# Output tiles of a two-layer hybrid transformer step: early tiles normed from DRAM by a task of their own, last head pair in token order

## The chip, the cores and the metric

The kernel runs on one core of one Trainium2 chip. The metric is the device time of one execution in microseconds (us), the median of several runs. Five engines work in parallel, each through its own instructions in order: TensorE (matrix products; PE in the profile, and PEld for its weight loads), VectorE (DVE), ScalarE (ACT), GpSimd (POOL) and SyncE (SP), which here only issues DMAs. Products write to PSUM, all else lives in SBUF, and DRAM is reached by DMA.

## The reference, cut to what matters

One inference step of a two-layer model on 1280 tokens: 256 context tokens and 1024 latent tokens, width 1024. In each layer

```
h   = rms_norm(x, g) * (1 + scale) + shift      # scale, shift, gate from SiLU(cond) @ mod_w
out = mixer(h)                                  # layer 0: attention and RWKV-7, layer 1: gated linear attention
x   = x + gate * (out @ w_out)
```

Layer 0 splits its projection into grouped-query attention (8 query heads, 2 key heads of 64, softmax; context tokens see 256 keys, latent tokens 1536 keys, 512 cached and 1024 latent) and a two-directional RWKV-7 recurrence; both are gated by SiLU, concatenated and put through one output projection `ev_w_out`. Layer 1 projects the new h to q, k, v, gate and decay inputs, runs chunked gated linear attention in both directions and projects with `od_w_out`. A last rms_norm gives the outputs, beside new keys, values and states. All is float32; the kernel writes each product as three products of a high and a low part (`hi*hi + lo*hi + hi*lo`).

## The kernel before, in words

**Tiles and groups.** The 1280 tokens are ten tiles of 128 (tiles 0 and 1 are the context) and three groups: group 0 is tiles 0 and 1, group 1 tiles 2 to 5, group 2 tiles 6 to 9.

**The planner.** The kernel is written as generator tasks in streams. `Sched.drive` runs all of them at build time: at each step it issues, among the instructions that stand next in some task, the one that by its cost numbers would start first (streams with a lower number first on ties). What it issues goes to the engines from one helper, line 357, so every row of the trace has L357, and each engine's order is fixed when the program is built. Tasks wait for conditions with `sch.until`, take buffer slots with `get` and give them back with `put`.

**Attention.** Twelve units, one for a head pair p4 (0 to 3) and a group, stand in a list (line 1668): for each head pair the groups 1, 2, 0. A unit finds the maxima of its scores (`mx`, sent through DRAM as `mr` into the row operand `QB`), multiplies `QA,KA` and `QB,KB` for scores, takes exponentials into `pt`, adds these up in `acc`, multiplies `pt,VO` for outputs and `acc,ones` for sums; their reciprocal `rcp` scales the gate path `ga`, which goes to the DRAM tensor `o`.

**Output tiles of layer 0** (`out_tile`, line 2191). A tile waits until its group is complete in `o` (attention and RWKV), loads its 128 tokens into the staging slot `wst` (one slot for the whole kernel, used for weight blocks as well), splits them into `oh` and `ol` (two slots each), and multiplies with the output weights `woh`, `wol`: 24 products for each block of 512 columns (tile 2: blocks of 256). At its first block it takes one of two slots `xt` and loads the residual x. `gt` is the product times the gate; `xt` becomes the sum, its squares go to `sq`, and `finish0` (line 2255) stores xt to the DRAM tensor `x1`. Three tiles may be under way at once, in the order of `TILES` (line 2272): tiles 2 to 9, then 0 and 1.

**The norm of the next layer.** `finish0` then waits for `flags["normed"]`, keeps its xt slot meanwhile, scales xt in place by the inverse root of `sq`, transposes it on TensorE (`ident,xt`), applies scale and shift into `xr` (one slot) and splits that into `h1hi`, `h1lo`. The room for these two is taken by attention, and `room_norm` opens it only when all twelve units are done. From then on the projections of layer 1 (`project`, line 1805) load their weights through wst into `whi`, `wlo` and multiply with h1hi, h1lo, group after group in the order 1, 2, 0.

Of the kernel before, what the change touches and what calls it, by code (L numbers as in the profile page):

```python
# [20 lines left out]
P = 128  # L21
DM = 1024
NK = DM // P
# [7 lines left out]
GROUPS = ((0, 256), (256, 512), (768, 512))  # L31
# [72 lines left out]
class Sched:  # L104
# [285 lines left out]
    def put(self, tag, tile):  # L390

        tile.slot.over = True
        self._release(tile.slot)
# [93 lines left out]
def tile_hybrid_dit_step(ctx: ExitStack, tc: tile.TileContext, I, C, O):  # L487
    nc = tc.nc
    sch = Sched(tc)
# [36 lines left out]
    def slots_in(pool0):  # L526
        def slots(tag, n, shape, dtype=F32, pool=None, fill=None):
            ts = [(pool or pool0).tile(shape, dtype, name=f"{tag}_{i}") for i in range(n)]
            for t in ts:
                if fill is not None:  # L530
                    G.memset(t, fill)
            sch.slots(tag, ts)
        return slots
# [190 lines left out]
    shared = slots_in(pool(ctx, "shared", side="right"))  # L724
    shared("wst", 1, [P, NK, P])
    shared("gt", 2, [P, 512])
    shared("sq", 6, [P, 4])
    shared("pj", 4, [P, 512], pool=pp)
    shared("a", 4, [P, 512], pool=pp)
    for tag in ("b", "po"):  # L730
# [934 lines left out]
    SLACK = 13  # L1665
    halves = [slice(64 * hh, 64 * hh + 64) for hh in range(2)]
    queries = {}
    units = [(p4, g) for p4 in range(4) for g in (1, 2, 0)]
    attended = [0, 0]

    def scores(g):
# [130 lines left out]
    heads = [dict(q={}, k={}, Vt={}, Sb={}, ready=set(), inner={}, back=set(), sf=None, out=0) for h in range(4)]  # L1802
    c128 = "p (c t) -> p c t"

    def project(cols, use):
        yield from sch.until(lambda: flags["normed"])
        yield from project_on(I["od_w_in"][0], H["hi"], H["lo"], cols, use, lambda g, a: normed[g] == GROUPS[g][1] // P, ORDER)

        def done():
            flags["units"] += 1  # L1810
        sch.then(done)
# [71 lines left out]
    def gates(h, u):  # L1883
        hd = heads[h]
        unit = 2 * h + u

        def use(g, t0, n, p):
            t1 = yield from get("gt", False)
            S.activation(out=t1[:, 0:n], in_=p, func=AF.Tanh, scale=0.5)
            V.scalar_tensor_tensor(out=t1[:, 0:n], in0=t1[:, 0:n], scalar=1.0, in1=p, op0=ALU.add, op1=ALU.mult)  # L1890
            D.dma_start(out=gg_d[g][:, unit, :], in_=t1[:, 0:n])
            put("gt", t1)

            def done():
                gated[g] += 1
            sch.then(done)
        yield from project([(0, OD_G + unit * P, P)], use)

    def step(h, d, tt, kt, Vt, j, cur, new):

# [290 lines left out]
    def out_tile(i, tt, src, finish):  # L2191
# [17 lines left out]
        copy(oh, ot)  # L2209
        pair(ol, ot, oh.bitcast(F32), ALU.subtract)  # L2210
        put("wst", ot)
        if i == 1:
            D.dma_start(out=xt, in_=src(tt))
        if tt in (0, 2):
# [2 lines left out]
            D.dma_start(out=gate, in_=gate_d[i][c:c + 1, :].to_broadcast([P, DM]))  # L2217
        yield from sch.until(lambda: (i, c) in gates_of)
        gate = gates_of[i, c]
        m = 256 if tt == 2 else 512  # L2220
        for b in range(DM // m):
            yield from sch.until(lambda: have[i] >= (b + 1) * m // P)
            cs = slice(b * m, (b + 1) * m)
# [25 lines left out]
        yield from finish(tt, xt, sq)  # L2249

    used = {}
    NW1 = 2
    MIXED = (8, 4)

    def finish0(tt, xt, sq):
        D.dma_start(out=x1_d[tt], in_=xt)
        yield from sch.until(lambda: flags["normed"])
        yield from norm_tile(1, tt, xt, sq, H["hi"], H["lo"])

        def done():  # L2260
            normed[0 if tt < 2 else (tt + 2) // 4] += 1
        sch.then(done)

    def finish1(tt, xt, sq):
        V.scalar_tensor_tensor(out=xt, in0=xt, scalar=sq[:, 2:3], in1=H["fg"], op0=ALU.mult, op1=ALU.mult)
# [8 lines left out]
    def room_proj():  # L2274
        yield from sch.until(lambda: all(x["over"] == 10 for x in sts))
        segs.close()
        out_pool(0, left, "wo0", 2)
        slots_in(pool(left, "xr", side="left"))("xr", 1, [P, NK, P])
        yield from move("b", "pj", 3)

    def room_norm():
# [70 lines left out]
    NAFTER = (0,0,0,6)  # L2352
    NGATE = 2
    def tiles(i):
        return ((out_tile(i, tt, (x_src, lambda t: x1_d[t])[i], (finish0, finish1)[i]) for tt in TILES), 3)

    def weights(i):
        return ((out_weights(i, (I["ev_w_out"], I["od_w_out"])[i][0], c) for c in range(8)), 2)
# [2 lines left out]
           ((states(h, g) for h in range(4) for g in (2, 1, 0)), 1, None, 0.15, 1.0),  # L2361
           ((outputs(h, g) for h in range(4) for g in ORDER), 2, None, 0.15, 1.0))
    sch.drive(([room_attn(), room_rwkv(), room_proj(), room_norm(), room_gla(), room_out(), room_more()], 7), *layer0_streams, *mixers,
              weights(0), tiles(0), *gla, (projections(), 2, None, 0.0, 1.5), weights(1), tiles(1))
    left.close()
    right.close()

# [82 lines left out]
```

## Time and profile before

| | before |
|---|---|
| median of 3 runs | 2095.14 us (2094.4 to 2097.18) |
| the profiled execution | 2095.28 us, span 2093.5 us |
| TensorE busy | 1997.0 us, 95% |
| VectorE, ScalarE, GpSimd busy | 1452.4, 1007.6, 289.9 us (69, 48, 14%) |
| weight loads on TensorE | 1557.7 us, 74% (beside the products) |
| TensorE busy from 1240 to 1470 us | 208.47 of 230 us |
| DMA | 219.56 MB, mean 105 GB/s |

The span is the time from the first to the last recorded instruction; the execution's own time has 1.8 us around it. A row of the trace gives start, duration, engine, line, operation and `output<-inputs` by the program's names; a bracket behind it is the engine's idle time ahead of the row and what ended it. Matmul rows overlap (a product of 512 columns shows 0.39 us, the next starts 0.23 us later), so the distance of starts is what one costs. The granted clock (PEclk) is a share of TensorE's upper level of 2.4 GHz; the lower level is 1.2 GHz.

### The profile page before, as it was taken

Reading aid. Unit: us, or ns where it says so; the run is one execution under the profiler, and the core shown is the slowest. Engines: PE = TensorE matmul, PEld = TensorE weight load, DVE = VectorE, ACT = ScalarE, POOL = GpSimd, SP = SyncE. Lnnn points to the kernel's source line nnn. Section 1 sums busy time; section 2 is a strip of 40 time slices with the busy share of each in tenths; the row PEclk is TensorE's granted clock in tenths of the full one; section 3 lists DMA queues with packets and bytes.
Section 4 is the critical chain, followed back from the end, with each engine's and each line's share of the span. In section 5 each row is a group of like instructions: output and inputs, shape, how many; then the busy total and the mean of one; then the engine's idle time right before and its main releaser. Section 6 shows DMA issues by size and latency. Waiting matters only on the chain.

```text
span 2093.5 us, 38539 instructions
## 1 busy us (share of the span) xinstructions
PE 1997.0 (95%) x14876; PEld 1557.7 (74%) x14876; DVE 1452.4 (69%) x2879; ACT 1007.6 (48%) x2184; POOL 289.9 (14%) x383
## 2 busy tenths in 40 slices
PE   6999999998999999999999999799999999999998
PEld 4878687886667777777776766578778888888886
DVE  4677866777887888778888987453575656564455
ACT  4454744553556655665656563333445454542111
POOL 2010200013221112121110020010121111110011
PEclk9999999999999999999999999899999999999999
DMA  8224342527513241323223224342102011115653
GB/s 297 71 101 159 138 164 81 179 91 238 170 54 103 81 143 59 97 74 111 78 68 88 67 70 143 95 146 73 50 14 64 28 50 29 49 31 165 192 170 112
DMA packets 215143, 219.56 MB, mean 105 GB/s; under 512 B 16480, under 2 KB 161232, under 8 KB 214960
## 3 DMA queue, kind: packets, MB, share of 16 engines
q1 hardware_dynamic: 214960, 217.10, 33.0%
q8 instruction: 117, 1.92, 0.4%
q14 instruction: 66, 0.54, 0.1%
HBM read 149.63 MB, written 67.39 MB: 104 GB/s over the span
## 4 chain that ended last, share of the span: by engine, by line
PE 52%; DVE 11%; issue 4%; ACT 3%; DMA 1%; POOL 0%; SPq 0%; POOLq 0%; DVEq 0%; ACTq 0%
PE a L357 26%; PE pj L357 26%; DVE QQ L357 2%; DVE LL L357 1%; DVE mx L357 1%; ACT QQ L357 1%; DVE TT L357 1%; DVE dec L357 1%; DVE gt L357 1%; DVE Z L357 1%; DVE y L357 1%; DVE GR L357 0%; DVE KX L357 0%; DVE GH L357 0%; DVE Ad L357 0%
## 5 line engine op out<-in xcount | busy, mean ns | idle before, releaser
L357 PE MATMUL pj<-hhi,whi 128*128 128x512 f32 (+1 forms) x672 | 241.1, 361 | 2.6 <-DVE whi L357 1.4
L357 PE MATMUL pj<-hhi,wlo 128*128 128x512 f32 (+1 forms) x672 | 240.4, 360 | 1.6 <-DVE wlo L357 1.6
L357 PE MATMUL pj<-hlo,whi 128*128 128x512 f32 (+1 forms) x672 | 241.3, 361 | 0.6 <-DVE hlo L357 0.6
L357 PEld LDWEIGHTS pj<-hhi,whi 128*128 128x128 f32 x672 | 128.9, 192 | 26.4 <-issue 3.7
L357 PEld LDWEIGHTS pj<-hhi,wlo 128*128 128x128 f32 x672 | 128.9, 192 | 24.0 <-issue 4.1
L357 PEld LDWEIGHTS pj<-hlo,whi 128*128 128x128 f32 x672 | 129.1, 192 | 23.7 <-issue 5.8
L357 POOL TENSOR_TENSOR acc<-acc,pt 128x512 f32<-128x512 f32 (+1 forms) x57 | 73.0, 1286 | 389.3 <-ACT pt L357 190.5
L357 PE MATMUL a<-h1hi,whi 128*128 128x512 f32 (+2 forms) x304 | 111.9, 369 | 0.0
L357 PE MATMUL a<-h1lo,whi 128*128 128x512 f32 (+2 forms) x304 | 111.0, 366 | 0.0
L357 PE MATMUL a<-h1hi,wlo 128*128 128x512 f32 (+1 forms) x296 | 109.9, 371 | 0.0
L357 PE MATMUL pj<-h1hi,whi 128*128 128x512 f32 (+2 forms) x296 | 108.4, 366 | 1.5 <-ACT h1hi L357 0.8
L357 PE MATMUL pj<-h1lo,whi 128*128 128x512 f32 (+2 forms) x296 | 108.4, 366 | 0.0
L357 PE MATMUL pj<-h1hi,wlo 128*128 128x512 f32 (+1 forms) x280 | 102.4, 366 | 0.0
L357 DVE TENSOR_TENSOR acc<-acc,pt 128x512 f32<-128x512 f32 (+1 forms) x127 | 90.6, 736 | 14.4 <-ACT pt L357 9.5
L357 PE MATMUL a<-pt,VO 128*64 128x512 f32 (+1 forms) x368 | 95.9, 605 | 0.0
L357 POOL TENSOR_SCALAR sq<-sq 128x1 f32<-128x1 f32 x70 | 19.9, 284 | 510.2 <-ACT gt L357 225.1
L357 DVE TENSOR_REDUCE mx<-pj 128x1 f32<-128x512 f32 (+1 forms) x118 | 75.4, 653 | 3.3 <-PE pj L357 3.1
L357 DVE TENSOR_REDUCE mx<-a 128x1 f32<-128x512 f32 x90 | 59.1, 669 | 10.8 <-PE a L357 10.7
L357 ACT ACTIVATE pt<-pj 128x512 f32<-128x512 f32 (+1 forms) x105 | 60.8, 597 | 10.2 <-PE pj L357 7.8
L357 PE MATMUL pj<-woh,oh 128*128 128x512 f32 (+1 forms) x160 | 61.5, 384 | 3.9 <-DVE oh L357 3.9
L357 PEld LDWEIGHTS a<-h1hi,whi 128*128 128x128 f32 (+1 forms) x304 | 56.9, 187 | 9.5 <-DVE gt L357 0.8
L357 PEld LDWEIGHTS pj<-h1hi,whi 128*128 128x128 f32 (+1 forms) x296 | 55.5, 188 | 11.2 <-ACT h1hi L357 1.2
(509 smaller groups left out, 5477.0 us busy)
## 6 DMA issues: line engine op xcount, KB each, us to landing
mw<-in_mod_w SPq DMA_DIRECT2D x24, 1024.0 KB
ws<-wk SPq DMA_DIRECT2D x32, 512.0 KB
wst<-in_ev_w_in SPq DMA_DIRECT2D x26, 512.0 KB
wst<-in_od_w_in SPq DMA_DIRECT2D x24, 512.0 KB
AR<-ws SPq DMA_DIRECT2D x40, 256.0 KB
BK<-ws SPq DMA_DIRECT2D x40, 256.0 KB
wst<-o SPq DMA_DIRECT2D x14, 512.0 KB
Vs<-vt SPq DMA_DIRECT2D x80, 64.0 KB
```

The costliest lines, as they stand in the source:

```text
L357: r = f(*a, **k)
```

## The change

Tiles that are finished before the room for h is open no longer keep their xt slot: `finish0` stores xt, gives the slot back and notes the tile in `rest`. A new task, `renorm`, waits for the room and goes through the tiles in token order; a noted tile it loads again from `x1` and norms. Tiles that finish later are normed at once as before. The last head pair's units and the tiles of layer 0 go in token order (groups 0, 1, 2). `project` waits until 8 tiles have split their activations, and the first two gate units (`NGATE`) project in the order 0, 1, 2. The tile with blocks of 256 columns is the first of its layer (tile 0 in layer 0, tile 2 in layer 1). `sq` has 12 slots in place of 6, `xr` 2 in place of 1.

```diff
@@ -724,7 +724,7 @@
     shared = slots_in(pool(ctx, "shared", side="right"))
     shared("wst", 1, [P, NK, P])
     shared("gt", 2, [P, 512])
-    shared("sq", 6, [P, 4])
+    shared("sq", 12, [P, 4])
     shared("pj", 4, [P, 512], pool=pp)
     shared("a", 4, [P, 512], pool=pp)
     for tag in ("b", "po"):
@@ -1665,7 +1665,7 @@
     SLACK = 13
     halves = [slice(64 * hh, 64 * hh + 64) for hh in range(2)]
     queries = {}
-    units = [(p4, g) for p4 in range(4) for g in (1, 2, 0)]
+    units = [(p4, g) for p4 in range(4) for g in ((1, 2, 0) if p4 < 3 else (0, 1, 2))]
     attended = [0, 0]
 
     def scores(g):
@@ -1802,9 +1802,9 @@
     heads = [dict(q={}, k={}, Vt={}, Sb={}, ready=set(), inner={}, back=set(), sf=None, out=0) for h in range(4)]
     c128 = "p (c t) -> p c t"
 
-    def project(cols, use):
-        yield from sch.until(lambda: flags["normed"])
-        yield from project_on(I["od_w_in"][0], H["hi"], H["lo"], cols, use, lambda g, a: normed[g] == GROUPS[g][1] // P, ORDER)
+    def project(cols, use, order=ORDER):
+        yield from sch.until(lambda: flags["normed"] and split[0] >= 8)
+        yield from project_on(I["od_w_in"][0], H["hi"], H["lo"], cols, use, lambda g, a: normed[g] == GROUPS[g][1] // P, order)
 
         def done():
             flags["units"] += 1
@@ -1894,7 +1894,7 @@
             def done():
                 gated[g] += 1
             sch.then(done)
-        yield from project([(0, OD_G + unit * P, P)], use)
+        yield from project([(0, OD_G + unit * P, P)], use, (0, 1, 2) if unit < NGATE else ORDER)
 
     def step(h, d, tt, kt, Vt, j, cur, new):
 
@@ -2209,6 +2209,10 @@
         copy(oh, ot)
         pair(ol, ot, oh.bitcast(F32), ALU.subtract)
         put("wst", ot)
+
+        def got():
+            split[i] += 1
+        sch.then(got)
         if i == 1:
             D.dma_start(out=xt, in_=src(tt))
         if tt in (0, 2):
@@ -2217,7 +2221,7 @@
             D.dma_start(out=gate, in_=gate_d[i][c:c + 1, :].to_broadcast([P, DM]))
         yield from sch.until(lambda: (i, c) in gates_of)
         gate = gates_of[i, c]
-        m = 256 if tt == 2 else 512
+        m = 256 if tt == 2 * i else 512
         for b in range(DM // m):
             yield from sch.until(lambda: have[i] >= (b + 1) * m // P)
             cs = slice(b * m, (b + 1) * m)
@@ -2249,17 +2253,38 @@
         yield from finish(tt, xt, sq)
 
     used = {}
+    split = [0, 0]
+    rest = {}
     NW1 = 2
     MIXED = (8, 4)
 
     def finish0(tt, xt, sq):
         D.dma_start(out=x1_d[tt], in_=xt)
-        yield from sch.until(lambda: flags["normed"])
+        if not flags["normed"]:
+            put("xt", xt)
+
+            def stored():
+                rest[tt] = sq
+            sch.then(stored)
+        else:
+            yield from norm0(tt, xt, sq)
+
+    def norm0(tt, xt, sq):
         yield from norm_tile(1, tt, xt, sq, H["hi"], H["lo"])
 
         def done():
             normed[0 if tt < 2 else (tt + 2) // 4] += 1
         sch.then(done)
+
+    def renorm():
+
+        yield from sch.until(lambda: flags["normed"])
+        for tt in range(10):
+            yield from sch.until(lambda: tt in rest or normed[0 if tt < 2 else (tt + 2) // 4] == (2, 4, 4)[0 if tt < 2 else (tt + 2) // 4])
+            if tt in rest:
+                xt = yield from get("xt")
+                D.dma_start(out=xt, in_=x1_d[tt])
+                yield from norm0(tt, xt, rest[tt])
 
     def finish1(tt, xt, sq):
         V.scalar_tensor_tensor(out=xt, in0=xt, scalar=sq[:, 2:3], in1=H["fg"], op0=ALU.mult, op1=ALU.mult)
@@ -2275,7 +2300,7 @@
         yield from sch.until(lambda: all(x["over"] == 10 for x in sts))
         segs.close()
         out_pool(0, left, "wo0", 2)
-        slots_in(pool(left, "xr", side="left"))("xr", 1, [P, NK, P])
+        slots_in(pool(left, "xr", side="left"))("xr", 2, [P, NK, P])
         yield from move("b", "pj", 3)
 
     def room_norm():
@@ -2352,7 +2377,7 @@
     NAFTER = (0,0,0,6)
     NGATE = 2
     def tiles(i):
-        return ((out_tile(i, tt, (x_src, lambda t: x1_d[t])[i], (finish0, finish1)[i]) for tt in TILES), 3)
+        return ((out_tile(i, tt, (x_src, lambda t: x1_d[t])[i], (finish0, finish1)[i]) for tt in (range(10), TILES)[i]), 3)
 
     def weights(i):
         return ((out_weights(i, (I["ev_w_out"], I["od_w_out"])[i][0], c) for c in range(8)), 2)
@@ -2361,7 +2386,7 @@
            ((states(h, g) for h in range(4) for g in (2, 1, 0)), 1, None, 0.15, 1.0),
            ((outputs(h, g) for h in range(4) for g in ORDER), 2, None, 0.15, 1.0))
     sch.drive(([room_attn(), room_rwkv(), room_proj(), room_norm(), room_gla(), room_out(), room_more()], 7), *layer0_streams, *mixers,
-              weights(0), tiles(0), *gla, (projections(), 2, None, 0.0, 1.5), weights(1), tiles(1))
+              weights(0), tiles(0), ([renorm()], 1), *gla, (projections(), 2, None, 0.0, 1.5), weights(1), tiles(1))
     left.close()
     right.close()
 
```

**The order on TensorE at the end of attention.** Before, these rows are the end of the last unit (64x256 outputs and sums of group 0), the norm transposes of a finished tile, and the first products of tile 4:

```order
L357 MATMUL a_145<-acc_3850,VO 64x256
L357 MATMUL a_145<-acc_3851,VO 64x256
L357 MATMUL a_145<-pt_3848,VO 64x256
L357 MATMUL a_145<-pt_3849,VO 64x256
L357 MATMUL pj_143<-acc_3850,ones_3830 64x256
L357 MATMUL pj_143<-acc_3851,ones_3830 64x256
L357 MATMUL pj_141<-ident,xt_12380 128x128 x4
L357 MATMUL a_146<-ident,xt_12380 128x128 x4
L357 MATMUL pj_142<-woh_12372,oh_12375 128x512
L357 MATMUL pj_142<-wol_12373,oh_12375 128x512
L357 MATMUL pj_142<-woh_12372,ol_12377 128x512
```

In the changed kernel the last scores, outputs and sums of the last unit (group 2) stand here, and behind them output products:

```order
L357 MATMUL pj_147<-QA_3842,KA_3832 128x512
L357 MATMUL pj_147<-QB_3846,KB_3834 128x512
L357 MATMUL pj_149<-QA_3843,KA_3832 128x512
L357 MATMUL pj_149<-QB_3847,KB_3834 128x512
L357 MATMUL a_151<-pt_3854,VO 64x512
L357 MATMUL a_151<-pt_3855,VO 64x512
L357 MATMUL pj_148<-acc_3856,ones_3836 64x512
L357 MATMUL pj_148<-acc_3857,ones_3836 64x512
L357 MATMUL a_153<-woh_12368,oh_12371 128x512
L357 MATMUL a_153<-wol_12369,oh_12371 128x512
L357 MATMUL a_153<-woh_12368,ol_12373 128x512
```

Before, the last sums are followed at once by transposes. Now 86 products of 512 columns (rows 9373 to 9458: both blocks of tile 2, the first of tile 3, 14 products of tile 4's first) stand between the last sums and the first transposes. The place where these begin, tile 2's norm between products of tile 4 and tile 3:

```order
L357 MATMUL a_152<-woh_12368,oh_12371 128x512
L357 MATMUL a_152<-wol_12369,oh_12371 128x512
L357 MATMUL pj_147<-ident,xt_12376 128x128 x4
L357 MATMUL pj_149<-ident,xt_12376 128x128 x4
L357 MATMUL a_153<-woh_12368,oh_12372 128x512
```

The next transposes, of tile 0 loaded again, stand 34 products later (row 9495); those of tiles 3, 1, 4, 5, 6, 7, 8 and 9 follow at rows 9516, 9548, 9556, 9610, 9669, 9712, 9772 and 9825.

**The order on SP around the room.** Before: activations to wst for tiles 3 and 4 (o01 is group 1), a weight block of layer 1 (in_od_w_in), the stores of tiles 2 and 3, the last attention output (o00), and the residuals, store and activations that follow:

```order
L357 DMA wst_0_131<-o01_106 128x8x128 x2
L357 DMA wst_0_131<-in_od_w_in 128x8x128
L357 DMA x1_2_116<-xt_1_12380 128x1024
L357 DMA x1_3_117<-xt_0_12379 128x1024
L357 DMA o02_107<-ga_0_3852 128x512
L357 DMA ga_0_3852<-ga3_96 128x256
L357 DMA xt_1_12380<-in_x_sample 128x1024
L357 DMA o00_105<-ga_0_3852 128x256
L357 DMA xt_0_12379<-in_x_sample 128x1024
L357 DMA x1_4_118<-xt_1_12380 128x1024
L357 DMA wst_0_131<-o01_106 128x8x128
L357 DMA xt_1_12380<-in_x_sample 128x1024
```

In the changed kernel, from the store of tile 0 on (x1_0):

```order
L357 DMA x1_0_114<-xt_1_12376 128x1024
L357 DMA xt_1_12376<-in_x_sample 128x1024
L357 DMA gate_0_12370<-gate0_69 128x1024
L357 DMA wst_0_131<-o01_106 128x8x128
L357 DMA x1_1_115<-xt_0_12375 128x1024
L357 DMA o02_107<-ga_0_3858 128x512
L357 DMA xt_0_12375<-x1_0_114 128x1024
L357 DMA wst_0_131<-o01_106 128x8x128
L357 DMA x1_2_116<-xt_1_12376 128x1024
L357 DMA xt_1_12376<-in_x_sample 128x1024
L357 DMA x1_3_117<-xt_1_12376 128x1024
L357 DMA wst_0_131<-o02_107 128x8x128
```

The stores of tiles 0 and 1 stand ahead of the last attention output (o02), and the reload of tile 0 right behind it; tile 1's (row 550) follows two rows after this piece. The first weight block of layer 1 has moved to row 556, behind the activations of tile 7. These two are the only reloads.

## Rows read from the trace of the kernel before

**Rows 1.** The page: span, busy times, and the 40 slices (tenths).

```profile
span 2093.5 us, 38539 instructions
PE 1997.0 (95%) x14876; PEld 1557.7 (74%) x14876; DVE 1452.4 (69%) x2879; ACT 1007.6 (48%) x2184; POOL 289.9 (14%) x383
...
PE   6999999998999999999999999799999999999998
...
PEclk9999999999999999999999999899999999999999
```

**Rows 2.** Windows from 1240 to 1470: busy of each engine, PEclk, DMA share, GB/s.

```profile
1260.00:1280.00 20.00, 16.42 (x59) 8.44 (x60) 16.01 (x27) 8.52 (x18) 0.00 (x0) 0.83 0.68 203
...
1340.00:1350.00 10.00, 7.82 (x22) 5.77 (x23) 4.74 (x7) 3.40 (x9) 0.00 (x0) 0.54 0.54 158
...
1410.00:1420.00 10.00, 7.63 (x32) 5.96 (x31) 5.50 (x8) 4.78 (x10) 0.00 (x0) 0.83 0.37 84
...
sum 230.00, PE 208.47 PEld 155.91 DVE 125.86 ACT 87.56 POOL 17.03; mean PE 20.85 PEld 15.59 DVE 12.59 ACT 8.76 POOL 1.70
```

**Rows 3.** TensorE's waits, 1230 to 1520: total us, times, longest us.

```profile
PE pj L357 <- DVE xt L357: 9.9, 2, 7.5
PE a L357 <- DMA QB<-mr: 3.0, 1, 3.0
PE pj L357 <- DVE mx L357: 2.0, 1, 2.0
PE pj L357 <- ACT xt L357: 2.0, 1, 2.0
...
PE a L357 <- DVE rcp L357: 1.0, 1, 1.0
PE pj L357 <- ACT h1hi L357: 0.8, 1, 0.8
...
PE pj L357 <- ACT whi L357: 0.7, 1, 0.7
PE pj L357 <- ACT gsq L357: 0.6, 1, 0.6
```

**Rows 4.** Timeline of TensorE around the longest wait: start us, us, instruction.

```profile
1333.12 0.40 PE L357 MATMUL pj<-woh,ol 128*128 128x512 f32 x1
1341.01 1.12 PE L357 MATMUL pj<-ident,xt 128*128 128x128 f32 x4 [7.50 <-DVE xt L357]
...
1344.11 0.80 PE L357 MATMUL pj<-woh,oh 128*128 128x512 f32 x1 [1.13 <-DVE oh L357]
...
1349.31 0.39 PE L357 MATMUL pj<-woh,ol 128*128 128x512 f32 x1
...
1352.07 0.39 PE L357 MATMUL pj<-woh,ol 128*128 128x512 f32 x1
```

**Rows 5.** Timeline of VectorE beside it.

```profile
1338.00 1.22 DVE L357 TENSOR_TENSOR wlo<-wst,whi 128x1024 fp32r<-128x1024 f32 x1
1340.20 0.75 DVE L357 TENSOR_SCALAR xt<-xt,sq 128x1024 f32<-128x1024 f32 x1 [0.98 <-DMA x<-xt]
1343.36 0.69 DVE L357 CAST oh<-wst 128x1024 fp32r<-128x1024 f32 x1 [2.41 <-DMA wst<-o]
```

**Rows 6.** Timeline of SP: when DMAs were issued.

```profile
1337.51 0.32 SPq L357 DMA_DIRECT2D x<-xt  x1
1339.25 0.53 SPq L357 DMA_DIRECT2D wst<-o  x1
...
1405.76 0.33 SPq L357 DMA_DIRECT2D gate<-gate  x1
```

**Rows 7.** The chain that ended last, around 1405 us: start us, us, what.

```profile
1405.04 0.70 DVE gt L357
...
1406.49 5.42 DMA x<-xt
...
1412.03 0.76 DVE xt L357
```

## The prediction

> **What bounds the kernel now.** I read the page's totals first: TensorE is busy 1997.0 us of a span of 2093.5 us, no other engine comes near, and the line of 40 slices shows nearly full slices from the second on, with one clear hole in the middle and a granted clock that falls only there [rows 1]. So the kernel is bound by TensorE, the change does not alter its number of products, and all it can move is that hole. Second I cut the stretch 1240 to 1470 us into windows: TensorE is busy 208.47 of 230 us, so 21.53 us are idle [rows 2]. The same windows have a clock below full, and that is a second loss: 0.17 x 20 = 3.4 us in 1260:1280 and 0.17 x 10 = 1.7 us in 1410:1420 [rows 2]. In 1340:1350, mostly at the lower level (1.2 GHz), I take it from the products: the 24 from 1344.11 to 1352.07 need 1352.07 - 1344.11 + 0.23 = 8.2 us, while 12 steps from 1349.31 to 1352.07 give 0.23 us each at the upper level, 5.5 us for 24; loss 2.7 us [rows 4]. The eight transposes ahead of them lose under 1 us more, which I leave out. Together 21.5 + 3.4 + 1.7 + 2.7 = 29.3 us can be won here and next to nothing elsewhere.
>
> Third, who ends the idle times [rows 3]: two waits on the scaled residual tile xt make 9.9 us, a handover between two attention units 3.0 + 2.0 us (the round trip of its maxima through DRAM), the start of the norms when the room opens 2.0 us, and small ones. The longest, 7.5 us, runs from 1333.5 to 1341.01 [rows 4]. It looks like one late vector instruction, but three things stand in a row. Tile 4's last product starts at 1333.12; its x1 store is issued at 1337.51 [rows 6]; the scaling, in place, starts at 1340.20 when the store has landed [rows 5]. And TensorE has no other product to do, because tile 5's activations were loaded only at 1339.25 [rows 6] and cast at 1343.36 [rows 5]: the one staging slot wst held a weight block of the next layer until its low part was made at 1338.00 [rows 5]. So the same gap ends in two waits, 7.5 us and then 1.1 us at 1344.11 [rows 4], and taking away the first alone would have left TensorE waiting to 1344 for the second. Behind both is one fact: tiles 2 and 3 are finished, hold both xt slots, and cannot be normed before the last attention unit frees the room for h; tile 4 then starts with nothing beside it.
>
> **The change, part by part.** (1) *Tiles finished early give their xt slot back* (`finish0`, `renorm`), and tiles 0 and 1 come first. In the new order only tiles 0 and 1 finish before the room opens, so only two reloads are added, 512 KB each, and nothing on TensorE. The reload of tile 0 stands on SP's queue behind the last attention output. After the last attention product 86 output products follow before the first transposes, which are tile 2's: 86 x 0.23 = 19.8 us [rows 4]. Tile 0's transposes come 34 products later. A load of this size took 1343.36 - 1339.25 = 4.1 us from issue to first use [rows 5, 6], so both reloads lie under other work. The 19.8 us also replace what was missing: room, moves of buffers and norm set-up now pass under products that need no room.
>
> The Trainium skill, "DMA: Bandwidth & Descriptors", section "Anatomy of one DMA — SWDGE (gpsimd) path", speaks against a trip through DRAM: each DMA has a fixed cost of about 2.0 us, mostly the receipt of the write, and "this can cause a surprisingly long delay especially when the write target is HBM". The trace agrees in kind: the x1 stores here take 2.7 us and once 5.42 us until the scaling may go [rows 5 to 7]. By the page's figure a store and a reload would add an estimated 4 us and the movement for each of two tiles if nothing covered them; the order puts more than 19 us of products over both, so my sum has nothing for them.
>
> (2) *The weight blocks of the next layer wait until 8 tiles have been split* (`split[0] >= 8`). This takes the weight out of wst's way: on SP the activations of tiles 4 to 7 now come ahead of the first such weight. The 1.1 us wait and the part of the 7.5 us behind it have no cause any more.
>
> (3) *What is late next: the norm of each tile.* From a tile's last product to its transposes run gate, add, store, scale. Tile 4: 1333.5 to 1341.01, 7.5 us [rows 4]; tile 9: 1405.04 to 1412.03 + 0.76, 7.8 us, in which the store took 5.42 us, issued right behind a 512 KB gate load of 1405.76 [rows 6, 7]. With a store of 2.7 us the latter chain is 5.1 us. In the new order I count the products between each tile's last and its transposes: 38 for tile 2 (8.7 us); 28 and one set of transposes (1.0 us) for tiles 3 and 4 (7.4 us); 34 for tile 5 (7.8); 43 for tile 6 (9.9); tile 7 about 6.7, tile 8 7.4, tile 9 6.9 us, with 256-column products at half the price. At 5.1 us for all chains the stalls are 0; at 7.8 us they are 0 + 0.4 + 0.4 + 0 + 0 + 1.1 + 0.4 + 0.9 = 3.2 us. The gate rows of the latent tokens are now loaded early, which takes away what delayed tile 9; but two reloads are in the traffic: I take 1.8 us, about the sum at tile 4's 7.5 us.
>
> (4) *Head pair 3 in token order.* The last attention unit is now one of 512 tokens and 12 key tiles in place of 256 tokens and 2. The handover remains, in the same form: maxima, their trip through DRAM, the first scores. It cost 2.0 + 3.0 us [rows 3] and 3.4 us of clock [rows 2], 8.4 us. Bounds: 0, if the two tiles of products that are now at hand fall into it, and 8.4. The order shows some 94 products of 256 columns right behind the unit's first eight scores, but not in the wait itself; I take 5.2 us. The unit's end (last exponential, last sums) cost 0 to 2.0 us (the wait at the room [rows 3]) plus a reciprocal of about 1 us; bounds 0 and 3.0, taken 2.0.
>
> (5) *Gate units 0 and 1 in the order (0, 1, 2), two xr slots, 12 sq slots.* They decide what stands beside the last norms. The waits on h1hi (0.8) and whi (0.7) and on gsq (0.6) [rows 3] I leave as they are: 2.1 us. After the last transposes 72 products of 512 columns and some smaller ones stand ahead of the first that wait for the decay, 72 x 0.23 = 16.6 us at least, so the last norm is not exposed.
>
> Sum of what is left: 5.2 + 2.0 + 1.8 + 2.1 = 11.1 us, against 29.3. Gain 18.2 us. The profiled execution took 2095.28 us (the span of 2093.5 and 1.8 around it), 0.14 us above the median of 2095.14, which I neglect: 2095.2 - 18.2 = **2077.0 us**. With all terms at their lower bounds 2.1 us stay, gain 27.2, 2068; with all at their upper bounds 8.4 + 3.0 + 3.2 + 2.1 = 16.7, gain 12.6, 2082.6.
>
> **Rivals.** *A, the residual slots become the new wait.* Two xt slots now carry ten tiles and two reloads. One of them serves tile 2, tile 3, the reloaded tile 1 and tile 5: from tile 2's transposes load 4.1, chain 7.8, reload, scale and transposes 5.9, load 4.1, chain 7.8: 29.7 us. TensorE has in that stretch 140 products and five sets of transposes, 32.2 + 5 = 37 us. For: each load waits for another tile's transposes, and SP issues in order, so the store of tile 3 stands ahead of the load for tile 4. Against: 7 us of slack. If loads and stores that overlap take twice as long (the store did: 5.42 against 2.7), the slot is 29.7 + 3 x 4.1 + 2.7 = 44.7 us, 7.7 us late, and the clock falls once more, about 2.7 us: 2077.0 + 10.4 = **2087**.
>
> *B, the hole moves.* The 86 products are only two and a half tiles' worth that now stand behind the attention instead of under its last unit, so that unit may run uncovered: its scores wait for exponentials as the old handover did. For: the old last unit had 8 scores of 256 columns and the tiles around it. Against: 94 + 48 products are still placed between its steps. A second handover (8.4 us) and tail (3.0) beyond my terms, with a clock loss of 3.4: 2077.0 + 14.8 = **2092**, no change.
>
> *C, slower: TensorE starves at several tiles.* Mechanism: the reload of an early tile takes an xt slot before its room on TensorE comes, the next tile's residual is not there, its sums fill the PSUM slots and the products behind stand still. Price of one such stop, from the gap of before: 7.5 + 1.1 + 2.7 = 11.3 us [rows 3, 4]. It decides from two on, which use up the gain: 2077.0 + 22.6 = **2099.6**; three would give 2111. For: the planner knows no such landing times as 5.42 us. Against: two reloads only, and the slack under A.
>
> **How the numbers follow.** Forecast (2068 to 2084, its own range) 0.70; A 0.15; B 0.08; C 0.07. About 0.2%, 4.2 us, is what a measurement of this kernel can tell from no change. The forecast and A are faster by more, B within, C beyond on the other side: faster 0.85, same 0.08, slower 0.07. The range is 2067 to 2090: it takes in the forecast's bounds and A.
>
> **What would show it.** In the new profile TensorE should be busy above 95% in every 100 us between 1200 and 1500, with no wait over 3 us behind xt, and the clock near full from the last attention product on; the reloads should be issued within 5 us of the last attention output and land long before their transposes. The handover's waits on mx and QB should be the largest that are left, together 3 to 4 us. A shows as waits of TensorE for xt whose vector instruction waits for a load; B as waits for pt, acc or mr around 1250 to 1300; C as two or more gaps above 7 us with a clock of 1.2 GHz behind each. If the idle time went as forecast and the time did not, the clock terms are wrong.

## The result and the profile after

The changed kernel takes 2078.68 us (median of 5 runs, 2075.22 to 2080.1) against 2094.49 us of the kernel before beside it: ratio 0.9922, 95% interval 0.9909 to 0.9936, so 15.8 us faster (13.4 to 19.1). The forecast was 2077.0.

The profiled execution has a span of 2077.7 us, 15.8 us less than before [rows 1]. The page:

```profile
span 2077.7 us, 38540 instructions
PE 1991.9 (96%) x14876; PEld 1554.9 (75%) x14876; DVE 1453.5 (70%) x2877; ACT 1007.2 (48%) x2181; POOL 296.1 (14%) x388
```

The hole of before is nearly gone: TensorE's busy share from 1300 to 1500 us is above 98%. What is left lies ahead of 1300, where 91.67% misses the prediction's sign of more than 95% in every 100 us. Windows (columns as in [rows 2]):

```profile
1200.00:1300.00 100.00, 91.67 (x621) 58.84 (x621) 85.07 (x143) 52.00 (x107) 16.52 (x9) 0.98 0.31 94
1300.00:1400.00 100.00, 98.18 (x484) 79.61 (x482) 56.36 (x84) 36.43 (x84) 10.88 (x18) 1.00 0.46 147
1400.00:1500.00 100.00, 98.80 (x542) 79.00 (x541) 43.74 (x72) 38.93 (x73) 7.73 (x11) 1.00 0.23 68
```

TensorE's waits from 1230 to 1520 us, which answer to [rows 3]:

```profile
PE pj L357 <- DVE mx L357: 5.3, 3, 3.2
PE a L357 <- DVE ol L357: 1.0, 1, 1.0
PE a L357 <- DVE QQ L357: 0.8, 1, 0.8
PE pj L357 <- ACT gsq L357: 0.6, 1, 0.6
PE pj L357 <- DVE xt L357: 0.6, 1, 0.6
```

The 9.9 us behind xt are 0.6, the 2.0 us at the room and the 3.0 us behind QB are gone, and the maxima (mx) have grown from 2.0 to 5.3 us, where the prediction's sign was 3 to 4 us on mx and QB together.

The reloads are covered. SP issues the load of tile 0 (xt<-x) 1.1 us after the last attention output (o<-ga), and that of tile 1 only 32 us after it, at 1356.92:

```profile
1324.70 0.32 SPq L357 DMA_DIRECT2D o<-ga  x1
1325.76 0.32 SPq L357 DMA_DIRECT2D xt<-x  x1
...
1335.91 0.61 SPq L357 DMA_DIRECT2D x<-xt  x1
...
1356.92 0.32 SPq L357 DMA_DIRECT2D xt<-x  x1
```

VectorE scales tile 0 at 1329.74, 4.0 us after the issue, tile 1 at 1361.76, 4.8 us after, and tile 2 at 1341.39, 5.5 us after its store was issued (1335.91), the link that the prediction read at 2.7 and 5.42 us:

```profile
1329.74 0.76 DVE L357 TENSOR_SCALAR xt<-xt,sq 128x1024 f32<-128x1024 f32 x1 [0.69 <-DMA xt<-x]
...
1341.39 0.75 DVE L357 TENSOR_SCALAR xt<-xt,sq 128x1024 f32<-128x1024 f32 x1 [5.52 <-DMA x<-xt]
...
1361.76 0.75 DVE L357 TENSOR_SCALAR xt<-xt,sq 128x1024 f32<-128x1024 f32 x1
```

On TensorE the last sums start at 1320.80, tile 2's transposes wait 0.55 us, and tile 0's come at 1350.87, 20 us after it was scaled. Tile 1's come at 1363.55, 1.0 us after it was scaled: no wait, but the prediction's sign (both reloads issued within 5 us of the last attention output, and landed long before their transposes) holds for tile 0 alone:

```profile
1320.80 1.13 PE L357 MATMUL pj<-acc,ones 128*64 128x512 f32 x3
...
1342.20 1.09 PE L357 MATMUL pj<-ident,xt 128*128 128x128 f32 x8 [0.55 <-DVE xt L357]
...
1350.87 0.38 PE L357 MATMUL pj<-ident,xt 128*128 128x128 f32 x2
...
1363.55 0.60 PE L357 MATMUL pj<-ident,xt 128*128 128x128 f32 x4
```

**A ruler for the rest.** The two programs give TensorE the same order up to head pair 3's first products. I measure from the last easily found products ahead of these (products of the recurrence, pj<-Z,TT followed by a<-TT,Z; before: 1155.00) to the first product of 64 rows of the next layer's decay inputs (before: 1463.25); the same number of products lies ahead of that one in every run. The kernel before needs 308.25 us for this stretch, the changed kernel 1448.31 - 1158.39 = 289.92: a gain of 18.3 us. In this profile 3.4 us were lost ahead of it, in code that is the same, and 0.9 us won behind it: 18.3 - 3.4 + 0.9 = 15.8.

### The profile page after: what moved, and what is told of

Same layout as the page of the kernel before. It is cut to its first block, busy times and chain, and to the rows that moved or that the text cites. A ratio compares the mean times of both kernels' runs of the same rounds, so it can differ in the third digit from the quotient of the medians.

```text
span 2077.7 us, 38540 instructions
## 1 busy us (share of the span) xinstructions
PE 1991.9 (96%) x14876; PEld 1554.9 (75%) x14876; DVE 1453.5 (70%) x2877; ACT 1007.2 (48%) x2181; POOL 296.1 (14%) x388
## 4 chain that ended last, share of the span: by engine, by line
PE 55%; DVE 11%; issue 2%; ACT 2%; DMA 1%; SPq 0%; POOL 0%; POOLq 0%; DVEq 0%; ACTq 0%
PE a L357 31%; PE pj L357 24%; DVE QQ L357 2%; DVE mx L357 1%; DVE LL L357 1%; ACT QQ L357 1%; DVE TT L357 1%; DVE Z L357 1%; DVE dec L357 1%; DVE gt L357 1%; DVE y L357 0%; DVE GR L357 0%; DVE KX L357 0%; DVE acc L357 0%; DVE TR L357 0%
## 5 line engine op out<-in xcount | busy, mean ns | idle before, releaser
L357 PE MATMUL a<-h1hi,whi 128*128 128x512 f32 (+3 forms) x448 | 162.2, 363 | 0.0
L357 PE MATMUL a<-h1lo,whi 128*128 128x512 f32 (+3 forms) x448 | 161.7, 362 | 0.4 <-DVE h1lo L357 0.4
L357 PE MATMUL a<-h1hi,wlo 128*128 128x512 f32 (+1 forms) x424 | 153.7, 362 | 0.0
L357 PE MATMUL a<-woh,oh 128*128 128x512 f32 (+1 forms) x248 | 91.8, 370 | 2.8 <-DVE oh L357 2.8
L357 PEld LDWEIGHTS a<-h1hi,whi 128*128 128x128 f32 (+1 forms) x448 | 83.3, 186 | 13.3 <-issue 0.4
L357 PEld LDWEIGHTS a<-h1lo,whi 128*128 128x128 f32 (+1 forms) x448 | 83.3, 186 | 13.2 <-DVE h1lo L357 0.8
L357 PE MATMUL a<-woh,ol 128*128 128x512 f32 (+1 forms) x248 | 91.5, 370 | 1.7 <-DVE ol L357 1.7
L357 PE MATMUL a<-wol,oh 128*128 128x512 f32 (+1 forms) x248 | 91.5, 369 | 0.0
L357 PEld LDWEIGHTS a<-h1hi,wlo 128*128 128x128 f32 x424 | 80.1, 189 | 11.2 <-DVE wlo L357 0.4
L357 ACT ACTIVATE pt<-pj 128x512 f32<-128x512 f32 (+1 forms) x123 | 68.7, 593 | 35.4 <-PE pj L357 31.8
```

The costliest lines, as they stand in the source:

```text
L357: r = f(*a, **k)
```

## The experiments

All ratios are to the kernel before on the same chip; the stretch is from the run's one profile.

| kernel | median, us | ratio, 95% interval | stretch, us |
|---|---|---|---|
| before | 2093.85 to 2096.18 | 1 | 308.25 |
| changed | 2078.68 | 0.9922, 0.9909 to 0.9936 | 289.92 |
| e1 renorm alone | 2121.04 | 1.0114, 1.0099 to 1.0130 | 330.77 |
| e2 wait for split tiles alone | 2095.05 | 1.0004, 0.9994 to 1.0015 | 307.87 |
| e3 order alone | 2080.92 | 0.9929, 0.9915 to 0.9942 | 292.52 |
| e4 changed, no renorm | 2081.40 | 0.9927, 0.9914 to 0.9939 | 291.68 |
| e5 units' order alone | 2094.33 | 0.9997, 0.9987 to 1.0008 | 304.48 |
| e6 tiles' order alone | 2097.47 | 1.0021, 1.0012 to 1.0031 | 309.92 |
| e7 before, split wait, 4 tile tasks | 2088.70 | 0.9975, 0.9966 to 0.9984 | 300.69 |
| e8 changed, maxima 20 ahead | 2079.11 | 0.9936, 0.9922 to 0.9951 | 295.60 |
| e9 changed again | 2077.31 | 0.9917, 0.9903 to 0.9930 | 289.98 |
| e10 changed, weights' low parts on VectorE | 2074.99 | 0.9911, 0.9899 to 0.9924 | 287.10 |
| e11 changed, no split wait | 2075.56 | 0.9912, 0.9899 to 0.9925 | 290.14 |
| e12 changed, maxima 16 ahead | 2080.75 | 0.9929, 0.9917 to 0.9942 | 291.56 |

The kernel before has one profile too. In 11 of the 13 runs its 308.25 us gives a larger gain than the ratio does, by 1.5 us on the mean of all 13, so gains read from the stretch may be too large by about that (an estimate). e5's 3.8 us is the clearest case: its interval allows 2.7 at most.

**e1: renorm alone.** The kernel before with `finish0`, `renorm` and 12 sq slots of the changed one:

```diff
-        yield from sch.until(lambda: flags["normed"])
+        if not flags["normed"]:
+            put("xt", xt)
...
-              weights(0), tiles(0), *gla, ...
+              weights(0), tiles(0), ([renorm()], 1), *gla, ...
```

> The kernel before with one part of the change alone: tiles finished early go to DRAM and are normed by a task of their own (renorm, 12 sq slots); units, tiles and projections keep the old order, the next layer's weights may still take wst. In the order 240 output products now stand ahead of the last sums and 80 behind them before the first transposes, but four tiles (2 to 5) are reloaded, and their transposes come at the very end, five sets in a row with hardly a product between. Theory (the hole closes where products are at hand, and opens where a chain load-scale-transposes has none): the wait of 7.5 us at the room goes, but a new stop of 8 to 13 us stands at the end of the norms; gain 3 to 8 us, 2087 to 2092. Rival 1 (the held xt slots are the whole cause): nearly the full gain, 12 to 18 us. Rival 2 (the gain is the order of units and tiles): 0 to 2 us.

Slower by 1.1%, 22.5 us in the stretch. The sign was against every theory, the mechanism was the first one's. Timeline of TensorE at the end of the norms:

```profile
1430.83 1.11 PE L357 MATMUL pj<-ident,xt 128*128 128x128 f32 x4 [5.81 <-DVE xt L357]
...
1436.56 1.11 PE L357 MATMUL pj<-ident,xt 128*128 128x128 f32 x4 [3.76 <-ACT xt L357]
...
1443.72 0.98 PE L357 MATMUL pj<-ident,xt 128*128 128x128 f32 x4 [3.49 <-DVE xt L357]
...
1447.96 1.09 PE L357 MATMUL pj<-ident,xt 128*128 128x128 f32 x4 [2.41 <-DVE xt L357]
...
1453.88 1.22 PE L357 MATMUL pj<-h1hi,whi 128*128 128x512 f32 x2 [3.98 <-ACT h1hi L357]
```

Five waits, 19.5 us: tile 1's own chain, then four early tiles that come back through two slots, with no product left to stand beside them (the granted clock is 0.51 from 1430 to 1440 us, nearly all at its lower level of 1.2 GHz). Two more waits, 7.0 us on oh at 1343.91 and 6.9 us on xt at 1399.70, are, as I read them, the old hole, moved. Releasing the slots is no gain by itself.

**e2: the split wait alone.** The kernel before with the count of split tiles and

```diff
-        yield from sch.until(lambda: flags["normed"])
+        yield from sch.until(lambda: flags["normed"] and split[0] >= 8)
```

> The kernel before with one part alone: projections wait until 8 tiles are split, so no weight block of the next layer holds the staging slot wst. Tile 5's products can then follow tile 4's at once, 18 of them ahead of tile 4's transposes (4.1 us) in place of none. Theory (two causes in a row behind the 7.5 us wait, wst being the second): the 7.5 + 1.1 us shrink to 3 to 4 us and the clock drop behind them mostly goes; gain 5 to 8 us, about 2088. Rival 1 (held xt slots are the whole cause): 1 us, the 1.1 us wait alone. Rival 2 (order): 0 to 2 us.

No change. The wait of 7.5 us at tile 4 is gone (its transposes come at 1347.24 without a wait), but other waits took its place; the waits of this run:

```profile
PE pj L357 <- DVE xt L357: 4.9, 3, 4.1
PE pj L357 <- ACT oh L357: 3.3, 1, 3.3
PE a L357 <- DMA QB<-mr: 2.8, 1, 2.8
PE pj L357 <- ACT whi L357: 2.2, 1, 2.2
```

The wait of 1.1 us on oh is now 3.3 us, and tile 5's low parts (ol) are late by 1.2 us:

```profile
1339.33 0.79 PE L357 MATMUL pj<-woh,oh 128*128 128x512 f32 x1 [3.31 <-ACT oh L357]
...
1414.23 1.12 PE L357 MATMUL pj<-ident,xt 128*128 128x128 f32 x4 [4.14 <-DVE xt L357]
```

The 4.1 us on xt are not what is left of the 7.5: that wait is tile 9's and was 2.4 us before. It and the weights that now come late (whi, 2.2 us in place of 0.7) use up most of what was won at tile 4. The theory's 3 to 4 us at that place were 4.5 us on oh and ol, and the clock still drops there (0.84 and 0.73 in the two windows from 1330 to 1350).

**e3: the order alone.** The kernel before with

```diff
-    units = [(p4, g) for p4 in range(4) for g in (1, 2, 0)]
+    units = [(p4, g) for p4 in range(4) for g in ((1, 2, 0) if p4 < 3 else (0, 1, 2))]
-        m = 256 if tt == 2 else 512
+        m = 256 if tt == 2 * i else 512
-    ... for tt in TILES), 3)
+    ... for tt in (range(10), TILES)[i]), 3)
```

> The kernel before with one part alone: the last head pair's units and layer 0's tiles in token order (and the 256-column blocks at tile 0); finished tiles keep their xt slot until the room is open, weights may take wst. 144 products stand under the last unit, none between the last sums and the transposes of tiles 0 and 1, then 91 products. Theory: the stop at the room stays at 3 to 5 us, the weight in wst makes tile 3 late by up to 3 us, handover and norms as in the changed kernel; gain 6 to 12 us, about 2085. Rival 1 (held xt slots are the whole cause): most of the hole stays, gain 0 to 4 us. Rival 2 (order is all): the full gain, 14 to 18 us.

Nearly the whole gain, 15.7 of 18.3 us of the stretch, and a ratio that the interval doesn't part from the changed kernel's. The theory's 6 to 12 us were too few, and "order is all" is right within 2.6 us, though tiles 0 and 1 hold both xt slots and a weight block holds wst across the room, as tiles 2 and 3 and a weight did before. TensorE at the room:

```profile
1322.96 1.76 PE L357 MATMUL pj<-ident,xt 128*128 128x128 f32 x12 [2.39 <-ACT xt L357]
1324.51 1.06 PE L357 MATMUL a<-ident,xt 128*128 128x128 f32 x4
...
1347.20 1.04 PE L357 MATMUL pj<-ident,xt 128*128 128x128 f32 x8
```

VectorE there, the weight's low part and tile 3's activations:

```profile
1329.67 1.23 DVE L357 TENSOR_TENSOR wlo<-wst,whi 128x1024 fp32r<-128x1024 f32 x1
...
1335.12 0.69 DVE L357 CAST oh<-wst 128x1024 fp32r<-128x1024 f32 x1 [1.86 <-DMA wst<-o]
```

The room costs 2.4 us (2.0 before). But behind it stand both blocks of tile 2, 48 products or 11 us, and tile 3's activations are cast at 1335.12, before these run out: no wait. Tile 2's own chain has 43 products beside it. Before, 24 products of one block stood there and the next activations came at 1343.36.

**e4: the changed kernel without renorm** (`finish0` of before, no `renorm` stream).

> The changed kernel without its main part: finished tiles wait for the room in their xt slots again, no renorm, no reload; order and the wait of the projections stay. Theory: only the stop between the last sums and the first transposes comes back, 3 to 5 us, so 2 to 5 us slower than the changed kernel, 2080 to 2084. Rival 1 (the held xt slots are the whole cause, as the prediction said): 10 us or more slower than the changed kernel, 2089 to 2095. Rival 2 (order is all): the same time as the changed kernel within 2 us.

By the times it can't be told from the changed kernel (0.9927 and 0.9922, 1 us); the stretch is 1.8 us longer, just under the theory's lower end and inside the 2 us of the second rival, "order is all". It is the wait at the room: 2.4 us as in e3, 0.55 us in the changed kernel. e4 has all of the change but renorm, so against e3 it also prices what was not tested alone (the gate units' order and the xr slots) together with the split wait: 0.8 us.

**e5 and e6: each half of the order.** e5 has only the first line of e3's edit, e6 only the other two.

> The kernel before with half of the order alone: head pair 3's units in the order 0, 1, 2; the tiles stay in the order 2 to 9, 0, 1. In the order 24 products of tile 4 follow the room as before, but 6 of tile 5 stand ahead of tile 4's transposes. Theory (what closes the hole is that two whole tiles of products are at hand when the room opens, and that comes from tiles 0 and 1 being the finished ones): the waits on xt and oh come back, within 4 us of the kernel before, 2090 to 2097. Rival (the old last unit of 256 tokens and its handover made the hole): 10 us or more faster than before, 2080 to 2086.

> The kernel before with the other half of the order alone: layer 0's tiles in token order (256-column blocks at tile 0); the units stay 1, 2, 0. No output product can stand under the last units (0 in place of 168 ahead of the last sums), all of them follow, 127 ahead of the first transposes, and no tile waits for the room. Theory (cover after the room): no wait of over 2 us on xt behind the room, but the last units, without products between them, wait for exponentials and sums, 3 to 10 us more than before; 2083 to 2092. Rival (the units' order is all): no gain, 2093 to 2098.

By the times e5 is the kernel before and e6 is 0.2% slower; the stretch has 3.8 us less and 1.7 us more, where both together have 15.7 less. In e5 the wait is back under another name. TensorE:

```profile
1330.72 1.09 PE L357 MATMUL pj<-ident,xt 128*128 128x128 f32 x8 [2.39 <-ACT xt L357]
...
1344.76 0.79 PE L357 MATMUL a<-woh,oh 128*128 128x512 f32 x1 [6.56 <-DVE oh L357]
```

VectorE:

```profile
1337.42 1.23 DVE L357 TENSOR_TENSOR wlo<-wst,whi 128x1024 fp32r<-128x1024 f32 x1
...
1344.02 0.69 DVE L357 CAST oh<-wst 128x1024 fp32r<-128x1024 f32 x1 [1.90 <-DMA wst<-o]
```

The 24 products of one block stand between the room and the next activations, which come 13 us after the first transposes; 6.6 us are missing. In e6 the context's tiles are first in line, but their attention unit is the last: no output product can start under attention, and TensorE waits for the first activations, then for the first chain:

```profile
1305.88 0.58 PE L357 MATMUL a<-woh,oh 128*128 128x256 f32 x1 [9.86 <-DVE oh L357]
...
1339.27 1.12 PE L357 MATMUL pj<-ident,xt 128*128 128x128 f32 x4 [7.54 <-DVE xt L357]
```

The theory for e6 was wrong: the loss is not in the last units but in the 9.9 us behind them, and the wait of 7.5 us on xt, which was to go, is there.

**e7: more tile tasks in the old order.** e2's edit and

```diff
-    ... for tt in TILES), 3)
+    ... for tt in TILES), 4 - i)
```

> The kernel before, old order, with the projections waiting for 8 split tiles and four tile tasks under way in place of three (layer 0), so that tile 5 can be loaded, split and multiplied while tiles 2 and 3 wait for the room: 24 more products stand under the last unit and 36 (8.3 us) between tile 4's last product and its transposes, where before there were none. Theory (the stop at tile 4 is want of products, whatever the cause): the waits of 7.5 and 1.1 us and the clock drop go, those at the last tiles stay; 8 to 11 us faster than before, 2085 to 2088. Rival 1 (only a new order of units and tiles helps): no change. Rival 2 (held xt slots are the cause): no change, since tiles 2 and 3 hold both slots as before.

A gain of 7.6 us in the stretch with the old order and both slots held; the times say 0.9975, 5 us. That is just under the theory's 8 us, and against both rivals: a fourth task lets tile 5 be split and multiplied while tiles 2 and 3 wait. The 7.5 us at tile 4 are gone, and the activations there come late by 0.7 and 1.5 us. The largest wait on xt, 3.9 us, is tile 9's, 2.4 us before:

```profile
1346.31 0.50 PE L357 MATMUL a<-woh,oh 128*128 128x512 f32 x1 [0.71 <-ACT oh L357]
...
1348.58 0.50 PE L357 MATMUL a<-woh,ol 128*128 128x512 f32 x1 [1.54 <-DVE ol L357]
...
1406.92 0.63 PE L357 MATMUL pj<-ident,xt 128*128 128x128 f32 x4 [3.88 <-DVE xt L357]
```

**e8 and e12: head pair 3's maxima earlier** (K is 20 and 16):

```diff
-                want = (...) * PACE - SLACK
+                want = (...) * PACE - (SLACK if p4 < 3 else K)
```

> The changed kernel with head pair 3's maxima allowed 20 key-tile steps ahead in place of 13, which moves the last unit's maxima out of the stretch in which TensorE waits for VectorE's maxima (5.3 us in three waits); the rest of the order is the same. Theory (these waits are VectorE behind in its queue at that place): they go, with the clock drop behind the longest; 4 to 7 us faster than the changed kernel, 2072 to 2075. Rival (VectorE is the bound of the whole stretch, the waits move ahead): within 2 us of the changed kernel.

> The changed kernel with head pair 3's maxima allowed 16 steps ahead in place of 13 (20 moved the wait to the exponentials and made the stretch 5.7 us longer in its profile). Theory (VectorE is the bound of 1240 to 1270 us, so maxima and additions only trade places): waits of 4 to 8 us in sum again, behind mx, acc or pt; within 3 us of the changed kernel. Rival (there is a best distance): the waits fall to 3 us or less; 2 to 5 us faster.

The waits on mx fall to 1.3 and 0.7 us and come back behind the exponentials and sums; the stretch is 5.7 and 1.6 us longer. That fits e8's rival and e12's theory: VectorE is the limit there, and its work only trades places. TensorE in e8:

```profile
1264.42 1.39 PE L357 MATMUL a<-pt,VO 128*64 128x512 f32 x2 [4.19 <-ACT pt L357]
...
1272.83 1.07 PE L357 MATMUL a<-acc,ones 128*64 128x512 f32 x2 [1.96 <-DVE acc L357]
```

By the times e8 can't be told from the changed kernel (0.9936 and 0.9922, the intervals overlap); its profile shows a loss in the stretch, with an early start (1152.39) to make up for it.

**e9: the changed kernel again.**

> The changed kernel once more, unaltered, beside the three that follow: how far one profile repeats. Measured from the last product before the two programs part (the recurrence's pair ahead of head pair 3's first transfer) to the first product of 64 rows of the next layer's decay inputs, the first profile gave 289.9 us, the kernel before 308.3. If that stretch is what the change moved, it comes out at 288 to 292 us again, while the start of the stretch may lie anywhere between 1152 and 1159 us as in the profiles so far. If the gain were spread over the program, the stretch would vary with the whole.

The stretch repeats to 0.06 us while its start lies at 1151.06 instead of 1158.39. I therefore take differences of a few us in the stretch as the programs' own, and differences ahead of it not; two profiles of one program don't show how far a third would lie.

**e10: the weights' low parts on VectorE**, in `out_weights`:

```diff
-        pair(wl[:, :, cs], s3, wh[:, :, cs].bitcast(F32), ALU.subtract)
+        V.tensor_tensor(wl[:, :, cs], s3, wh[:, :, cs].bitcast(F32), ALU.subtract)
```

> The changed kernel with the low parts of the output weights always made on VectorE: GpSimd made two of the eight, 2.8 and 3.6 us each, from 1258.7 on, and while they ran one VectorE addition of 0.68 us took 2.86 us, ahead of the maxima that TensorE waited 3.2 us for. The order on TensorE is the same but for one pair of neighbours. Theory (the two engines hold each other up): the addition takes 0.7 us again, the longest wait on the maxima falls from 3.2 us to under 2 in spite of 2.4 us more work on VectorE; 0 to 3 us faster than the changed kernel. Rival (VectorE is simply full there): the waits grow by the 2.4 us; 1 to 3 us slower.

The theory holds: the longest wait on the maxima falls from 3.18 to 0.64 us, the stretch to 287.10, 2.9 us less than the changed kernel's and the shortest of all. The medians (2074.99 against 2077.31 for e9 beside it) point the same way, but their intervals overlap, so that it beats the changed kernel is shown by the profile and not by the times.

**e11: the changed kernel without the split wait** (e2's edit undone).

> The changed kernel without the wait of the projections for 8 split tiles; order, reloads and all else stay. A weight block may hold wst again ahead of tile 4 or 5. Theory (with the new order two tiles and four blocks of products lie between, so a late wst is covered): within 3 us of the changed kernel, stretch 290 to 293 us. Rival (wst is the second half of the gap, as the prediction has it): a wait on oh of 3 us or more comes back and the clock drops behind it; 5 to 9 us slower.

290.14 us, the same, though weight blocks take wst at 1314.56 and 1337.74, on both sides of the room; no wait on oh or ol comes. With the new order the split wait does nothing that can be measured.

## Why the prediction was right, and where it was not

The total was right: 18.2 us forecast, 18.3 us in the stretch, 15.8 us (13.4 to 19.1) by the times. The gap that closed is the one that was named. What carries the gain is not what I said, and that the number came out so near is in part luck.

- *"Behind both is one fact: tiles 2 and 3 ... hold both xt slots"* is false as the cause. Held slots cost 1.8 us (e4 to changed), the 2.4 us wait at the room less 0.55; releasing them in the old order costs 22.5 us (e1). With them held and the order new the gap closes (e3), and with them held and the order old 7.6 us are won by one more task and the split wait, which alone is worth 0.4 (e7, e2).
- *Part 1, reloads covered:* right, by 20 us of other work for tile 0 but by 1.0 us for tile 1. The 2.0 us that the prediction cites from the Trainium skill ("DMA: Bandwidth & Descriptors", section "Anatomy of one DMA — SWDGE (gpsimd) path") are those of the GpSimd path, and SyncE issues the DMAs here: no run tests them.
- *Part 2, the split wait:* "have no cause any more" held only because of the order. Alone it is worth 0.4 us (e2), on top of the order 0.2 us (e11). It also moved the conflict to tile 8, the first that it doesn't protect: tile 8's activations are issued at 1390.03 behind two weight blocks (1375.92, 1381.71), and TensorE waits 1.0 us for their ol at 1397.60, a wait that neither e3 nor e11 has. The sum had no term for it.
- *The order*, which I priced only by its handover, carries 15.7 us, and only with both halves (e5, e6). The 86 products that I put to the account of renorm are the right reading of the right cause: two blocks at hand when the room opens where there was one. I had them under the wrong edit, because I never asked what the order would do with the slots still held.
- *Part 3, norm chains, taken 1.8 us:* xt 0.6 and h1lo 0.4 us are 1.0.
- *Part 4, handover, taken 5.2 us:* 5.3 us idle and a dip of the clock, 0.96 over 1240:1280 in e9, 1.6 us. It was mis-sized by 1.7 us and has another cause: the round trip of the maxima through DRAM no longer ends a wait; VectorE is behind (e8, e10, e12). The same three waits on mx, 5.3 us, stand in e5, so the units' order brings them. *The unit's end, taken 2.0 us:* 0.5 us.
- *Part 5, taken 2.1 us:* 0.6 us (gsq); h1hi and whi are gone.
- *Sum of what is left, 11.1 us:* 1.0 + 1.0 (ol) + 6.9 + 0.5 + 0.6 = 10.0. The errors of -0.8, +1.0, +1.7, -1.5 and -1.5 us nearly cancel, and that is luck. 29.3 - 10.0 = 19.3 is 1.0 us more than the stretch's 18.3. Of that 0.9 lies ahead of 1230, where the sum did not look: TensorE idles 1.6 us from 1155 to 1230 before and 2.5 us from 1158.39 to 1233 now, among the products of the recurrence.
- *Rival C's* mechanism, reloads that find no product beside them, is real: it is e1. In the changed kernel only two tiles are reloaded and early ones; the order keeps C away. *A* and *B* did not come: 0.6 us on xt, behind a store, and 0.5 us on pt.

Why both halves are needed I argue from e5 and e6: the tiles that finish before the room must be ones whose attention is done early (units in token order), and they must be the first in line (tiles in token order), so that what stands behind the room is a whole tile of two blocks. That the planner left 48 products there and not 24 is read from the order; that 24 are too few here and 48 enough is shown by e3, e5 and the kernel before.

## What to carry to other kernels

Judge a gap by the work that stands beside the chain that it waits for, counted in products from the order, and not by the buffer that the waiting task holds. Price each edit with the others left out before crediting the gain to the one that the change is named after. When a program's runs scatter by as much as an edit is worth, measure the stretch between two instructions that both programs share.

## What the runs showed of the hardware

**The same code starts the stretch up to 7.3 us apart.** Its start lay between 1151.06 and 1158.39 us in 14 profiles. One place where the clock differs, windows 740 to 770 us, the changed kernel's first profile:

```profile
740.00:750.00 10.00, 8.94 (x62) 7.33 (x60) 8.68 (x14) 2.57 (x6) 3.44 (x4) 0.83 0.24 67
750.00:760.00 10.00, 8.10 (x107) 6.10 (x107) 9.91 (x25) 4.16 (x14) 0.00 (x0) 0.95 0.36 99
760.00:770.00 10.00, 9.91 (x72) 7.80 (x71) 5.27 (x14) 3.51 (x8) 0.00 (x0) 0.54 0.62 195
```

And its second profile, e9, with the granted clock at 1.00 throughout:

```profile
740.00:750.00 10.00, 8.58 (x99) 6.41 (x98) 10.00 (x20) 3.38 (x12) 1.18 (x3) 1.00 0.42 120
750.00:760.00 10.00, 8.35 (x104) 6.68 (x101) 9.91 (x27) 3.96 (x10) 0.00 (x0) 1.00 0.26 69
760.00:770.00 10.00, 8.96 (x123) 6.86 (x119) 8.10 (x19) 4.69 (x13) 1.04 (x1) 1.00 0.80 252
```

The order is the same and TensorE idles less in the first (3.1 us against 4.1); in one execution the clock was lowered there and in the other not. Why is open.

**A GpSimd instruction held up VectorE.** In the changed kernel GpSimd ran two subtractions of weights from 1258.72 to 1265.1:

```profile
1258.72 6.39 POOL L357 TENSOR_TENSOR wol<-xt,woh 128x1024 fp32r<-128x1024 f32 x2
```

VectorE's four additions beside it took 5.03 us:

```profile
1261.83 5.03 DVE L357 TENSOR_TENSOR acc<-acc,pt 128x512 f32<-128x512 f32 x4
```

In e10, without them, the same four took half as long:

```profile
1259.24 2.48 DVE L357 TENSOR_TENSOR acc<-acc,pt 128x512 f32<-128x512 f32 x4
```

The longest single addition between 1240 and 1275 us is 2.86 us in the changed kernel and 1.03 us in e10, the median 0.68 us in both. In e9 and e11, where GpSimd makes the two subtractions as well, it is 2.86 and 2.87 us. The Trainium skill, "SBUF — State Buffer", section "SBUF: two separate sides", says that a VectorE operation with two SBUF inputs and a GpSimd operation that reads SBUF exclude each other for a whole instruction; the 2.86 us agree with that. The long addition starts at 1262.80, 0.5 us after the second subtraction (1262.29, 2.82 us), and ends at 1265.66, 0.55 us after that ends.
